# A decoder trunk on one Trainium2 core: Strassen products moved ahead of the memory's keys and values, memory outputs gated later on GpSimd, pooling issued in steps

## The chip, the core and the metric

The kernel runs on one core of a Trainium2 chip. The metric is the device time of one execution in microseconds (us), lower is better. A profile of one execution shows five engines: TensorE (PE, with its weight loads apart as PEld), VectorE (DVE), ScalarE (ACT), GpSimd (POOL) and SyncE (SP), which issues every transfer of this kernel. Each engine works through its own instructions in order.

## What is computed

Two layers over 1024 tokens of 1024 channels, all in float32. Layer 0 is the one that the change touches:

```python
h = x @ w_in                       # 1024 x 3072
u_main, q_mem = h[:, :1024], h[:, 1024:1536]
g_main, g_mem = h[:, 1536:2560], h[:, 2560:]
# pooling: 4 groups of 256 channels, trailing mean over w = 2, 4, 8, 16 tokens
pm     = trailing_mean(u_main, w) - u_main
y_main = (pm @ pool_w[group]) * pool_scale
# memory: 4 heads of 128, 256 memory tokens
y_mem  = softmax(q_mem @ mk.T / sqrt(128)) @ mv      # mk, mv = mem @ w_mem_kv
y      = concat(y_main * silu(g_main), y_mem * silu(g_mem)) @ w_out
x      = layer_norm(alpha * x + y)
```

Layer 1 has the same memory branch and projection, and forgetting attention of 16 heads instead of the pooling.

## The kernel before

Every float32 product is made of three matmuls on pairs of a rounded high half and a low remainder (`hi_lo`, L139 to L142: a cast on ScalarE, L141, and a subtraction on VectorE, L142). Activations lie with channels on the 128 partitions and tokens along the free axis.

Layer 0's projection is computed in **pairs** of 128-channel slabs by Strassen's scheme in Winograd's form (`winograd`, L194 to L246): seven products of 12 matmuls of 512 columns (L215) instead of eight. The right operands are x's four quarters and four sums of them, T1 to T4, made once by `sums_of_x` (L452 to L462: 16 subtractions on GpSimd, then 16 `hi_lo`). The left operands are a pair's weight quarters and four sums of these on GpSimd (L233 to L245), each split by `hi_lo` into two of the six `w` buffers. The first pair of slabs (`first_pair`, L464 to L486) has 96 plain matmuls (L478), because the sums of x are not there yet. There are eleven further pairs: one for the memory's queries (`mem_queries(2)`), six for gates (`gates_out` writes silu gates, doubled, to `gd` in DRAM; `pool_gates` either loads them or computes them in place), four for the pooled channels (`pool_in`).

`mem_kv` (L255 to L286) makes the memory's keys and values: 96 matmuls of 256 columns (L270) and 48 of 512 (L280), with weights cast and subtracted on the way (`split_w`, L151 and L152). `mem_attention` (L301 to L365) goes over eight blocks of 128 tokens: scores into the PSUM tile `L` (L171), exponentials and scalings on ScalarE (L321, L327), transposes (L294), and for each two blocks and each head a value product into `O`, which has one bank. `took` (L545) takes it out of `O`. Between these steps the `Fill` object issues matmuls of two gate pairs.

`pooled` (L554) makes a group's trailing mean on VectorE by log2(w) shifted additions of 1024 columns (L561) for each of two slabs, then subtracts, splits, and `pool_out` (L590) multiplies by the group's 256x256 weights (24 matmuls of 512 columns, L171 into `L`) and by the gate (L606) and stores to `y0d`. `out_proj` (L366) loads `y0d` by 512 KB tiles, chunk 2 (memory) first, then 0 (groups 0 and 1), then 1 (groups 2 and 3), and multiplies by w_out (L394).

What sets the order: TensorE's instructions of layer 0 stand in the order of the program text (`manual_schedule`); those of the other engines and the transfers are put in an order by a scheduler at build time, with the program text as priority, and buffers handed out in that order. The pools that matter have few buffers: `G` 4, `T` 6, `raw` 3, `raw2` 4, `P` 4, `Y` 2, `w` 6 and PSUM `pj` 3, `L` 2, `T` 2, `O` 1. A tile that finds no free buffer waits on its engine until one is released.

Of the kernel before, what the change touches and what calls it, by code (L numbers as in the profile page):

```python
# [16 lines left out]
P = 128  # L17
S = 1024
# [49 lines left out]
def trunk_kernel(ctx, tc, x, xT, memT, win, wk, wv0, wv, wmk, wmv, wout, poolw, pscale, lng, lnb, bforget, out):  # L68
# [25 lines left out]
    def sb(shape, tag, bufs, dt=F32, where=None):  # L94
        return (where or pool).tile(shape, dt, tag=tag, name=nm(tag), bufs=bufs)
# [7 lines left out]
    def T(shape=(P, S), dt=F32R):  # L103
        return sb(list(shape), "T", 6, dt)
# [4 lines left out]
    def raw(shape):  # L109
        return sb(list(shape), "raw", 3)  # L110
# [80 lines left out]

    SLAB = 48 * NH

    def winograd(w, X, banks, temps, out):  # L194

        f32, spare = temps

        def load(d, pc, t):
            nc.sync.dma_start(t, w[d][pc])
            return t

        def split(t):
            h, l = wt([P, 4, P]), wt([P, 4, P])
            hi_lo(h, l, t)
            return h, l

        def product(name, t, took):  # L210
            (h, l), (xh, xl) = split(t), X[name]
# [9 lines left out]
        def add(dst, a, b):  # L221
            nc.vector.tensor_tensor(dst, a, b, ALU.add)

        left, right = slice(0, NH), slice(NH, S)
        u = spare()
        u2, u3 = u[:, 0, :], u[:, 1, :]
        a11 = load(0, 0, f32())
        yield from product("B11", a11, lambda acc: nc.scalar.copy(u2, acc))
        a12 = load(0, 1, f32())
        yield from product("B21", a12, lambda acc: out(0, left, acc, u2))  # L230
        a21, a22 = load(1, 0, raw([P, 4, P])), load(1, 1, raw([P, 4, P]))
        s1, s2 = f32(), f32()
        nc.gpsimd.tensor_tensor(s1, a21, a22, ALU.add)  # L233
        nc.gpsimd.tensor_tensor(s2, s1, a11, ALU.subtract)
        yield from product("T2", s2, lambda acc: add(u2, acc, u2))
        nc.gpsimd.tensor_tensor(a21, a11, a21, ALU.subtract)
        yield from product("T3", a21, lambda acc: add(u3, acc, u2))
        yield from product("T4", a22, lambda acc: out(1, left, acc, u3))

        def fifth(acc):  # L240
            add(u2, acc, u2)
            out(1, right, acc, u3)

        yield from product("T1", s1, fifth)
        nc.gpsimd.tensor_tensor(s2, a12, s2, ALU.subtract)  # L245
        yield from product("B22", s2, lambda acc: out(0, right, acc, u2))  # L246

    PAIR = 84 * NH

# [182 lines left out]
    with tc.tile_pool(name="in0", bufs=1) as in0:  # L432
# [17 lines left out]
        place = (("B11", "T4"), ("B21", "B22"))  # L450

        def sums_of_x():  # L452
            for k in range(4):
                (b11, b12), (b21, b22) = ((t[:, 0, :], t[:, 1, :]) for t in (quarters[k], quarters[4 + k]))
                t12, t34 = (T((P, 2, NH), F32) for _ in range(2))
                t1, t2, t3, t4 = t12[:, 0, :], t12[:, 1, :], t34[:, 0, :], t34[:, 1, :]
                nc.gpsimd.tensor_tensor(t1, b12, b11, ALU.subtract)
                nc.gpsimd.tensor_tensor(t2, b22, t1, ALU.subtract)
                nc.gpsimd.tensor_tensor(t3, b22, b12, ALU.subtract)
                nc.gpsimd.tensor_tensor(t4, b21, t2, ALU.subtract)  # L460
                for n, t in (("T2", t2), ("T3", t3), ("T1", t1), ("T4", t4)):
                    hi_lo(X[n][0][:, k, :], X[n][1][:, k, :], t)  # L462

        def first_pair():  # L464

            accs = [[ps([P, NH], *b) for b in banks] for banks in ((("pj", 3), ("pj", 3)), (("pj", 3), ("L", 2)))]
            ws = {}
            for kt in range(KT):
                for d in range(2):
                    if kt % 4 == 0:  # L470
                        ws[d] = split_w(win[0, 8 + d, kt // 4], [P, 4, P])
                    if d == 0:
                        load_x(kt)
                    h, l = ws[d]
                    for n in range(2):
                        xh, xl = X[place[kt // 4][n]]
                        for i, (a, b) in enumerate(((h, xh), (h, xl), (l, xh))):
                            nc.tensor.matmul(  # L478
                                accs[d][n], a[:, kt % 4, :], b[:, kt % 4, :],
                                start=kt == 0 and i == 0, stop=kt == KT - 1 and i == 2,  # L480
                            )
            for d in range(2):
                for n in range(2):
                    t = T((P, 2, NH))
                    hi_lo(t[:, 0, :], t[:, 1, :], accs[d][n])
                    nc.sync.dma_start(qd[:, :, d, n * NH : (n + 1) * NH], t.bitcast(F32))  # L486

# [17 lines left out]

        qd = dram.tile([P, 2, MH, S], F32, name="qd")
        gd = dram.tile([P, 12, S], F32, name="gd")

        def mem_queries(h0):
            def out(d, cols, acc, add):  # L510
# [32 lines left out]
            return [(t[:, 0, h, :], t[:, 1, h, :]) for h in range(MH)]  # L543

        def took(c, h, acc):  # L545
            cols = slice(c * 2 * P, (c + 1) * 2 * P)
# [3 lines left out]
            nc.vector.tensor_tensor(chunk[0][:, h, :], acc, chunk[1][:, h, :], ALU.mult)  # L550
            if h == MH - 1:
                nc.sync.dma_start(y0d[2, :, :, cols], chunk[0])

        def pooled(g, us):  # L554

            w = WINDOWS[g]
            for u in us:
                cur, sh = u, 1
                while sh < w:
                    nxt = G()  # L560
                    nc.vector.tensor_tensor(nxt[:, sh:], cur[:, sh:], cur[:, : S - sh], ALU.add)  # L561
                    nc.vector.tensor_copy(nxt[:, :sh], cur[:, :sh])
                    cur, sh = nxt, 2 * sh
                pm = G()
                nc.vector.scalar_tensor_tensor(pm[:, w - 1 :], cur[:, w - 1 :], 1.0 / w, u[:, w - 1 :], ALU.mult, ALU.subtract)
                nc.vector.tensor_tensor(pm[:, : w - 1], cur[:, : w - 1], invc[:, : w - 1], ALU.mult)
                nc.vector.tensor_tensor(pm[:, : w - 1], pm[:, : w - 1], u[:, : w - 1], ALU.subtract)
                ph, pl = T(), T()
                hi_lo(ph, pl, pm)
                yield ph, pl  # L570

        def pool_in(g):
            us = [sb([P, S], "P", 4) for _ in range(2)]

            def out(d, cols, acc, add):
                nc.vector.tensor_tensor(us[d][:, cols], acc, add, ALU.add)

            run(pair(2 * g, out))
            return us

        def pool_gates(g):
            ys = [sb([P, S], "Y", 2, F32, in0) for _ in range(2)]
            if g < 2:
# [6 lines left out]
        def pool_out(g, pms, ys):  # L590
            r = raw([P, 2, 2 * P])
            nc.sync.dma_start(r, poolw[g])
            wh, wl = (MK([P, 2, 2 * P]) for _ in range(2))
            hi_lo(wh, wl, r)
            for d in range(2):
                f = 2 * g + d
# [382 lines left out]
```

## Time and profile before

| | before |
|---|---|
| runs, us | 1390.39, 1389.15, 1387.25; median 1389.15 |
| profiled execution, us | 1387.68, span 1386.0 |
| TensorE busy | 1317.9 us (95%) |
| VectorE, ScalarE, GpSimd busy | 834.2, 580.4, 366.6 us |
| mean granted TensorE clock | 0.983 |
| first pair | 5.65 to 28.1 us |
| memory's keys and values | 40.64 to 77.2 us |
| three pairs | 77.22 to 134.5 us |
| memory attention with two pairs | 139.38 to 230.9 us |
| pooling, six pairs | 230.90 to 371.15 us |

Times inside the profiled execution count from the start of its span. A group row gives line, engine, operation, tile written <- tiles read, then time; in square brackets stands the idle time of the engine ahead of the instruction and what ended it. The wait views count the same idle times by what was waited for. A granted clock of 1.00 is full speed.

### The profile page before, as it was taken

What the parts mean: (1) busy time and instruction counts of PE and PEld (TensorE: products, weight loads), DVE (VectorE), ACT (ScalarE), POOL (GpSimd) and SP (SyncE); (2) the same over time, 40 slices, a digit from 0 to 9 for tenths busy, and PEclk for the clock granted to TensorE, in tenths of its full rate; (3) what the DMA queues carried; (4) which work ended last, traced back from release to release, by engine and by line L of the source; (5) the groups of instructions that cost most, each with busy time, mean ns of one, the idle gap of its engine ahead of it and who ended that gap; (6) DMA issues with size and microseconds to landing.
All of it is one profiled execution on the core that took longest, in us unless ns stands there. A gap on an engine that the chain in (4) does not pass through costs nothing. (4 is left out here: it accounts for less than half of the span.)

```text
span 1386.0 us, 19391 instructions
## 1 busy us (share of the span) xinstructions
PE 1317.9 (95%) x6830; PEld 1108.0 (80%) x6830; DVE 834.2 (60%) x1675; ACT 580.4 (42%) x1239; POOL 366.6 (26%) x448
## 2 busy tenths in 40 slices
PE   7598889999999999999999999999999999999997
PEld 5477777787778888888988888888888888878886
DVE  5967645998856555255545555555555656675553
ACT  4543644223341124266325555555555555563110
POOL 0732111313000000000025455454545454622000
PEclk9799889999999999999999999999999999999999
DMA  7343444231473325111422132222222132365431
GB/s 250 107 160 114 129 139 143 71 120 54 152 251 119 106 98 171 47 31 30 149 63 70 54 92 75 78 83 64 90 57 90 54 92 70 114 199 191 136 121 46
DMA packets 82498, 148.29 MB, mean 107 GB/s; under 512 B 7904, under 2 KB 33760, under 8 KB 82400
## 3 DMA queue, kind: packets, MB, share of 16 engines
q1 hardware_dynamic: 82400, 147.04, 33.5%
q8 instruction: 54, 0.88, 0.3%
q14 instruction: 44, 0.36, 0.1%
HBM read 107.56 MB, written 31.06 MB: 100 GB/s over the span
## 5 line engine op out<-in xcount | busy, mean ns | idle before, releaser
L183 PE MATMUL pj<-A,w 128*128 128x512 f32 x1824 | 494.3, 402 | 0.8 <-DVE MK L142 0.8
L183 PEld LDWEIGHTS pj<-A,w 128*128 128x128 f32 x1824 | 320.6, 189 | 51.6 <-DVE MK L142 1.2
L142 DVE TENSOR_TENSOR T<-T,T 128x512 fp32r<-128x512 f32 (+2 forms) x248 | 151.9, 637 | 174.7 <-ACT T L141 117.6
L215 PE MATMUL pj<-A,w 128*128 128x512 f32 x924 | 219.8, 395 | 3.4 <-DVE w L142 3.4
L215 PEld LDWEIGHTS pj<-A,w 128*128 128x128 f32 x924 | 174.1, 191 | 39.5 <-DVE w L142 4.5
L141 ACT CAST T<-T 128x512 fp32r<-128x512 f32 (+2 forms) x252 | 131.2, 549 | 137.2 <-DMA T<-y1d 46.3
L807 ACT ACTIVATE P<-P,s 128x128 f32<-128x128 f32 (+7 forms) x128 | 99.6, 778 | 141.5 <-DVE s L805 140.6
L798 POOL TENSOR_SCALAR P<-R,cumn 128x128 f32<-128x128 f32 (+7 forms) x128 | 96.8, 756 | 210.8 <-PE T L294 153.1
L294 PE MATMUL T<-ident,P 128*128 128x128 f32 x704 | 101.5, 273 | 1.8 <-DVE V L142 1.1
L294 PEld LDWEIGHTS T<-ident,P 128*128 128x128 f32 x704 | 84.9, 140 | 20.8 <-DVE T L142 1.4
L141 ACT CAST w<-raw 128x512 fp32r<-128x512 f32 x81 | 50.3, 623 | 114.9 <-PE pj L215 103.1
L840 PEld LDWEIGHTS O<-T,V 128*128 128x128 f32 x640 | 85.0, 190 | 11.4 <-DVE T L142 5.2
L171 PE MATMUL L<-B,B 128*128 128x512 f32 (+3 forms) x384 | 89.0, 339 | 1.1 <-DVE s L805 1.1
L840 PE MATMUL O<-T,V 128*128 128x256 f32 (+1 forms) x640 | 85.3, 278 | 3.0 <-DVE T L142 2.7
L709 POOL MEMSET G<- 128x128 f32 x1 | 0.2, 206 | 322.2 <-DVE V L657 322.2
L171 PEld LDWEIGHTS L<-B,B 128*128 128x128 f32 x384 | 71.6, 188 | 17.1 <-DVE s L805 1.7
L805 DVE CUSTOM_DVE_ANT_0 P<-L,P 128x512 f32<-128x512 f32 (+3 forms) x128 | 72.7, 568 | 14.5 <-PE L L171 11.0
L152 DVE TENSOR_TENSOR w<-raw,w 128x512 fp32r<-128x512 f32 x58 | 45.5, 786 | 47.3 <-ACT w L151 47.1
L152 POOL TENSOR_TENSOR w<-raw,w 128x512 fp32r<-128x512 f32 x54 | 70.2, 1299 | 4.4 <-PE pj L183 0.9
L142 DVE TENSOR_TENSOR w<-raw,w 128x512 fp32r<-128x512 f32 x81 | 64.0, 792 | 11.2 <-ACT w L141 10.8
L846 DVE TENSOR_TENSOR G<-O,G 64x256 f32<-64x256 f32 x64 | 27.0, 422 | 71.6 <-ACT G L845 70.8
L151 ACT CAST w<-raw 128x512 fp32r<-128x512 f32 x58 | 36.0, 622 | 57.5 <-PE pj L183 26.9
(210 smaller groups left out, 1945.9 us busy)
## 6 DMA issues: line engine op xcount, KB each, us to landing
raw<-in_win_dram SPq DMA_DIRECT2D x96, 256.0 KB, 2.7
raw<-in_wout_dram SPq DMA_DIRECT2D x48, 256.0 KB, 3.1
B<-B SPq DMA_DIRECT2D x64, 128.0 KB, 2.5
R<-cumd SPq DMA_DIRECT2D x16, 512.0 KB, 3.7
y0d<-Y SPq DMA_DIRECT2D x12, 512.0 KB, 3.5
T<-y0d SPq DMA_DIRECT2D x12, 512.0 KB, 4.0
T<-y1d SPq DMA_DIRECT2D x12, 512.0 KB, 4.2
qd<-T SPq DMA_DIRECT2D x8, 512.0 KB, 3.8
```

Source lines behind the costliest of these rows:

```text
L141: nc.scalar.copy(hi, src)
L142: nc.vector.tensor_tensor(lo, src, hi.bitcast(F32), ALU.subtract)
L151: nc.scalar.copy(h, r)
L152: (nc.gpsimd if low[0] else nc.vector).tensor_tensor(l, r, h.bitcast(F32), ALU.subtract)
L171: nc.tensor.matmul(acc, a, b, start=i == 0, stop=i == len(terms) - 1)
L183: nc.tensor.matmul(accs[n], a[:, k, :], b[:, kt, n * NH : (n + 1) * NH], start=kt == 0 and i == 0, stop=kt == KT - 1 and i == 2,)
L215: nc.tensor.matmul(acc, a[:, k, :], b[:, k, :], start=k == 0 and i == 0, stop=k == 3 and i == 2)
L294: nc.tensor.transpose(t[:, j, :], src[:, (4 * g + j) * P : (4 * g + j + 1) * P], ident)
L798: nc.gpsimd.tensor_scalar(p[:, :L], R[:, :L], 1.0, cumn[:, i * HEADS + hd : i * HEADS + hd + 1], ALU.mult, ALU.add)
L805: nc.vector.tensor_tensor_reduce(p[:, lo:up], lg, p[:, lo:up], 1.0, top, ALU.add, ALU.min, m[:, n : n + 1])
L807: nc.scalar.activation(p[:, :L], p[:, :L], AF.Exp, bias=top, scale=-1.0, accum_out=sums[:, 8 * (hd % 2) + i : 8 * (hd % 2) + i + 1])
L840: nc.tensor.matmul(acc[:, w:], st, t[j // 4][:, j % 4, w:], start=j == 0 and e == 0, stop=j == last and e == 1,)
```

## The change

The order of layer 0 becomes: first pair, sums of x (T1 and T2 for all four k ahead of T3 and T4), memory queries, gates of group 3, pooled channels of group 3, gates 4 (memory), pooling of group 3 to its end, queries prefetched, keys and values, memory attention with gates 5 (memory) and gates of group 2 as filling, pooled channels of groups 2 and 1, group 2's output, memory outputs, gates of group 1, pooled channels of group 0, outputs of 1 and gates and output of 0. Before, it was first pair, keys and values, sums, queries, gates 4 and 5, memory attention with gates of groups 0 and 1 as filling, then groups 0 to 3.

- `winograd` issues all four weight loads at its start and splits each product's weights one product ahead; T1 comes ahead of T4.
- `took` only copies `O` to a `Y` tile on ScalarE and stores it to a new DRAM tensor `yraw`; `mem_out` later loads it and the gates in `G` tiles and multiplies them on GpSimd.
- `pooled` becomes a generator with a stop after each step; after each Strassen product two steps of it are issued (`chore(2)`), and `pool_out` finishes what is left.
- The first pair's query tiles go to the `Y` buffers instead of `T`, and the pooling weights to `w` instead of `MK`.

```diff
+    chores = []
+    def chore(n):
+        while n and chores:
+            if next(chores[0], chores) is chores:
+                chores.pop(0)
+            else:
+                n -= 1
...
+        a11, a12 = load(0, 0, f32()), load(0, 1, f32())
+        a21, a22 = load(1, 0, raw([P, 4, P])), load(1, 1, raw([P, 4, P]))
...
+        ahead = split(steps[0][1]())
+        for j, (name, _, took) in enumerate(steps):
+            (h, l), (xh, xl) = ahead, X[name]
+            if j < 6:
+                ahead = split(steps[j + 1][1]())
             acc = ps([P, NH], *banks)
...
                         took(acc)
+                        chore(2)
...
-                    t = T((P, 2, NH))
+                    t = sb([P, 2, NH], "Y", 2, F32R, in0)
...
-                chunk[0], chunk[1] = sb([P, MH, 2 * P], "Y", 2, F32, in0), G((P, MH, 2 * P))
-                nc.sync.dma_start(chunk[1], gd[:, 8:, cols])
-            nc.vector.tensor_tensor(chunk[0][:, h, :], acc, chunk[1][:, h, :], ALU.mult)
+                chunk[0] = sb([P, MH, 2 * P], "Y", 2, F32, in0)
+            nc.scalar.copy(chunk[0][:, h, :], acc)
             if h == MH - 1:
-                nc.sync.dma_start(y0d[2, :, :, cols], chunk[0])
+                nc.sync.dma_start(yraw[:, :, c * 2 * P : (c + 1) * 2 * P], chunk[0])
+        def mem_out():
+            for h in range(MH):
+                y, gt = G(), G()
+                nc.sync.dma_start(y, yraw[:, h, :])
+                nc.sync.dma_start(gt, gd[:, 8 + h, :])
+                for cols in (slice(0, NH), slice(NH, S)):
+                    nc.gpsimd.tensor_tensor(y[:, cols], y[:, cols], gt[:, cols], ALU.mult)
+                nc.sync.dma_start(y0d[2, :, h, :], y)
...
         first_pair()
-        kv = mem_kv(0)
         sums_of_x()
...
         run(mem_queries(2))
-        for f in (4, 5):
-            run(gates_out(f))
-        for f in (0, 1):
+        run(gates_out(3))
+        pms = pool_in(3)
+        run(gates_out(4))
+        pool_out(3, pms, pool_gates(3))
+        queries(0)
+        kv = mem_kv(0)
+        for f in (5, 2):
             fill.add(gates_out(f), PAIR)
         mem_attention(kv, queries, fill, took)
-        pms = list(pooled(0, pool_in(0)))
-        for g in range(4):
-            us = pool_in(g + 1) if g < 3 else None
-            pool_out(g, pms, pool_gates(g))
-            if g < 3:
-                pms = list(pooled(g + 1, us))
+        pms2 = pool_in(2)
+        pms1 = pool_in(1)
+        pool_out(2, pms2, pool_gates(2))
+        mem_out()
+        ys = pool_gates(1)
+        pms0 = pool_in(0)
+        pool_out(1, pms1, ys)
+        pool_out(0, pms0, pool_gates(0))
```

More of the change, by code (lines that the diff above doesn't have):

```diff
@@ L208, in split, with add, less, sums @@
             return h, l
-        def product(name, t, took):
-            (h, l), (xh, xl) = split(t), X[name]
+        def add(dst, a, b):
+            nc.vector.tensor_tensor(dst, a, b, ALU.add)
+        def less(dst, a, b):
+            nc.gpsimd.tensor_tensor(dst, a, b, ALU.subtract)
+            return dst
+        left, right = slice(0, NH), slice(NH, S)
+        u = spare()
+        u2, u3 = u[:, 0, :], u[:, 1, :]
+        a11, a12 = load(0, 0, f32()), load(0, 1, f32())
+        a21, a22 = load(1, 0, raw([P, 4, P])), load(1, 1, raw([P, 4, P]))
+        s1, s2 = f32(), f32()
+        def sums():
+            nc.gpsimd.tensor_tensor(s1, a21, a22, ALU.add)
+            return less(s2, s1, a11)
+        def fifth(acc):
+            add(u2, acc, u2)
+            out(1, right, acc, u3)
+        steps = (
+            ("B11", lambda: a11, lambda acc: nc.scalar.copy(u2, acc)),
+            ("B21", lambda: a12, lambda acc: out(0, left, acc, u2)),
+            ("T2", sums, lambda acc: add(u2, acc, u2)),
+            ("T3", lambda: less(a21, a11, a21), lambda acc: add(u3, acc, u2)),
+            ("T1", lambda: s1, fifth),
+            ("T4", lambda: a22, lambda acc: out(1, left, acc, u3)),
+            ("B22", lambda: less(s2, a12, s2), lambda acc: out(0, right, acc, u2)),
+        )
+        ahead = split(steps[0][1]())
[3 more added lines that the diff above has]
+                ahead = split(steps[j + 1][1]())
             acc = ps([P, NH], *banks)
@@ L218, in product @@
                         took(acc)
+                        chore(2)
                     yield NH
[L221 to L246, printed above, removed]
     PAIR = 84 * NH
@@ L452, in sums_of_x @@
         def sums_of_x():
+            t12s = []
             for k in range(4):
                 (b11, b12), (b21, b22) = ((t[:, 0, :], t[:, 1, :]) for t in (quarters[k], quarters[4 + k]))
[L455 to L456 removed]
+                t12s.append(T((P, 2, NH), F32))
+                t1, t2 = (t12s[k][:, j, :] for j in range(2))
                 nc.gpsimd.tensor_tensor(t1, b12, b11, ALU.subtract)
                 nc.gpsimd.tensor_tensor(t2, b22, t1, ALU.subtract)
+                for n, t in (("T2", t2), ("T1", t1)):
+                    hi_lo(X[n][0][:, k, :], X[n][1][:, k, :], t)
+            for k in range(4):
+                (b11, b12), (b21, b22) = ((t[:, 0, :], t[:, 1, :]) for t in (quarters[k], quarters[4 + k]))
+                t34 = T((P, 2, NH), F32)
+                t3, t4 = t34[:, 0, :], t34[:, 1, :]
                 nc.gpsimd.tensor_tensor(t3, b22, b12, ALU.subtract)
[L460 to L461 removed]
+                nc.gpsimd.tensor_tensor(t4, b21, t12s[k][:, 1, :], ALU.subtract)
+                for n, t in (("T3", t3), ("T4", t4)):
                     hi_lo(X[n][0][:, k, :], X[n][1][:, k, :], t)
@@ L507, in trunk_kernel @@
         gd = dram.tile([P, 12, S], F32, name="gd")
+        yraw = dram.tile([P, MH, S], F32, name="yraw")
         def mem_queries(h0):
@@ L563, in pooled @@
                     cur, sh = nxt, 2 * sh
+                    yield
                 pm = G()
@@ L578, in pool_in @@
             run(pair(2 * g, out))
-            return us
+            pms = []
+            chores.append(pooled(g, us, pms))
+            return pms
         def pool_gates(g):
             ys = [sb([P, S], "Y", 2, F32, in0) for _ in range(2)]
-            if g < 2:
+            if g > 1:
                 for d in range(2):
@@ L590, in pool_out @@
         def pool_out(g, pms, ys):
+            while len(pms) < 2:
+                chore(1)
             r = raw([P, 2, 2 * P])
             nc.sync.dma_start(r, poolw[g])
-            wh, wl = (MK([P, 2, 2 * P]) for _ in range(2))
+            wh, wl = (wt([P, 2, 2 * P]) for _ in range(2))
             hi_lo(wh, wl, r)
```

7 lines of the change are left out of this document (4 added, 3 removed).

## Prediction

> **What bounds the kernel now.** I read the page's sections 1 and 2 first, then TensorE's waits over the whole span, then stages, then timelines. Section 1's engines and section 2's rows of TensorE and its clock:
>
> ```profile
> PE 1317.9 (95%) x6830; PEld 1108.0 (80%) x6830; DVE 834.2 (60%) x1675; ACT 580.4 (42%) x1239; POOL 366.6 (26%) x448
> PE   7598889999999999999999999999999999999997
> ...
> PEclk9799889999999999999999999999999999999999
> ```
>
> The longest of TensorE's waits (total, times, longest):
>
> ```profile
> PE O L171 <- DVE Y L550: 13.0, 6, 6.5
> PE pj L270 <- ACT w L151: 12.3, 1, 12.3
> PE pj L270 <- DVE w L152: 9.3, 7, 2.5
> PE L L171 <- DMA G<-qd: 4.9, 1, 4.9
> ```
>
> TensorE sets the end, and its waits of any size lie in slices 1 to 10, layer 0, which is all that the change touches. The stages of that layer:
>
> ```profile
> 28.00:77.00 49.00, 27.27 (x146) 22.43 (x145) 40.25 (x45) 23.80 (x44) 25.46 (x16) 0.83 0.46 145
> 77.00:134.00 57.00, 57.00 (x253) 47.22 (x252) 40.87 (x55) 22.55 (x37) 19.56 (x15) 1.00 0.40 130
> 139.00:231.00 92.00, 78.00 (x425) 66.85 (x426) 54.41 (x115) 50.40 (x136) 10.30 (x8) 0.90 0.43 134
> 231.00:371.00 140.00, 133.57 (x577) 108.60 (x576) 120.76 (x178) 43.03 (x67) 32.60 (x20) 0.99 0.30 97
> ```
>
> After the window come length, busy time of PE, PEld, DVE, ACT, POOL, granted clock, DMA share and GB/s. Both programs have 6822 matmuls, so I count each stage's **excess**, its time less its matmuls at full clock: 0.227 us for 512 columns (252 in 57.28 us), 0.141 for 256 (24 in 3.39). Memory keys and values: 28.1 to 77.2 is 49.1, work 96x0.141 + 48x0.227 = 24.4, excess 24.7. The wait for queries: 4.9. Memory attention: 139.4 to 230.9 is 91.5; work 168x0.227 + 8x1.43 for scores + 16x0.72 for values + 8x0.79 for transposes = 67.3; excess 24.2, of which 13.5 are waits and the rest mostly the clock after them. Pooling: 230.9 to 371.15 is 140.3, work 576x0.227 = 130.8, excess 9.5. Together 63.3 us to win from.
>
> **The start.** The memory's keys and values leave the place after the first pair, and with them the waits of 12.3 and 8.4 us on L270. The next pair's products stand there instead. What is late next is VectorE: in the built order the low half of that pair's first weights stands behind all 16 sums of x and their splits, two evacuations too. The fifth x tile, with which the second-quarter sums can begin, lands at 12.2 (ACT's cast of G). From there VectorE has 33 operations of 512 columns up to that split, GpSimd 15 subtractions or additions that it waits for or competes with. What they cost each other is in these rows, VectorE's three and then GpSimd's two:
>
> ```profile
> 41.56 1.75 DVE L142 TENSOR_TENSOR A<-T,A 128x512 fp32r<-128x512 f32 x1
> 43.23 0.68 DVE L152 TENSOR_TENSOR w<-raw,w 128x512 fp32r<-128x512 f32 x1
> 43.83 1.75 DVE L142 TENSOR_TENSOR A<-T,A 128x512 fp32r<-128x512 f32 x1
> ...
> 41.16 1.59 POOL L458 TENSOR_TENSOR T<-G,T 128x512 f32<-128x512 f32 x1
> 43.38 1.66 POOL L459 TENSOR_TENSOR T<-G,P 128x512 f32<-128x512 f32 x1 [0.63 <-DVE A L142]
> ```
>
> Beside a GpSimd operation VectorE steps 1.68 us, in GpSimd's gap 0.62: they take turns, and one GpSimd operation costs VectorE 1.06. So the split ends at 12.2 + 33x0.62 + 15x1.06 = 48.6. Bounds: 12.2 + 33x0.62 + 2 + 15x0.15 = 37 if GpSimd costs almost nothing (its own 15 operations at 1.29 end at 31.6), 52 if it costs a whole 1.29. I take 48.6, since both queues are full there as in the rows. The Trainium skill, SBUF — State Buffer, section Who interferes with whom, has the loser blocked until the whole other instruction ends. By that the price is 1.29 and the split ends at 52.0, not 48.6; the rows show 1.06, and I keep them. The first pair itself, without waits now after 6.4, will stutter behind the same queue (its last x split is VectorE's 27th operation, near 35) and end near 41; that is inside the 48.6. After a TensorE gap of that length the clock is half:
>
> ```profile
> 193.00:196.00 3.00, 0.00 (x0) 0.00 (x0) 0.95 (x2) 0.46 (x1) 0.00 (x0) 0.50 0.93 296
> 196.00:199.00 3.00, 2.78 (x10) 2.49 (x11) 0.59 (x2) 0.00 (x0) 0.00 (x0) 0.50 0.35 122
> 199.00:202.00 3.00, 3.00 (x12) 2.61 (x11) 0.68 (x2) 0.62 (x1) 0.00 (x0) 0.50 0.00 0
> ```
>
> Work of 3.3 took 6.1 us after the 6.5 us wait, and 4.6 for 2.9 after one of 2.1. I add 2.5. Excess 48.6 - 28.1 + 2.5 = 23.0.
>
> **Keys and values in their new place.** They stand after pool_out(3). Their second weight load waits on the sync queue behind the store of pool_out(3)'s last output, then takes 2.5 us to land, 0.6 + 0.7 to split; 12 matmuls of the first weight cover 1.7. That leaves 3.6, with clock and the eight value slabs (0.8 and 0.3 waited in layer 1) 6.0; bounds 1 and 9.
>
> **Memory attention.** Queries are prefetched ahead of the keys: the 4.9 goes, with 2.6 of slow clock after it. The product of gates goes from VectorE (L550, 0.42) and its gate load with it; a copy on ScalarE takes its place (L845 shows such a copy from O). The one-bank tile O is still freed before the next head. In the built order ScalarE copies head 0, then four exponentials, a tanh and four scalings, then head 1. After head 0's matmuls end at 188.7 that queue ran:
>
> ```profile
> 188.80 0.47 ACT L321 ACTIVATE P<-L,s 128x256 f32<-128x256 f32 x1 [1.69 <-PE O L171]
> 190.61 0.64 ACT L501 ACTIVATE G<-G 128x512 f32<-128x512 f32 x1
> 191.24 1.71 ACT L327 ACTIVATE P<-P,s 128x256 f32<-128x256 f32 x4
> ```
>
> So with head 0's copy (0.45) ahead, head 1's ends at 194.0, while TensorE is ready for head 2 at 191.5: 2.6 us, in three of four chunks, each with 1.5 of slow clock; bounds 0 and 4.3. The Trainium skill, TensorE: Matmul & The Clock Gate, Part 1, lets the clock fall only after an idle window of about 3.4 us. By it the 1.5 would be nothing here and the sum 4.5 lower; the trace has 0.50 at 346 to 348 after a wait of 2.13, though not after one of 2.28 at 363. The last chunk keeps its 2.9, and I let 2.5 of today's unexplained rest stay: 3x4.1 + 2.9 + 2.5 = 17.7.
>
> **Pooling.** VectorE's pooling of group 3 is 12 operations of 1.14 (1024 columns), small ones 1.5; gates pair 4, beside it, brings 18 of 0.64. Before, two pairs were there to hide it. Now pool_out(3) follows one pair (19.1): VectorE needs 13.7 + 1.5 + 11.5 + 4 GpSimd operations at 0.75 = 30, and stays busy until then, so TensorE waits first for the last weights, then for the pooled tile: 11.7 with clock, bounds 8 and 14. Group 2 beside pair 1 the same way: 20.2 + 3 against 19.1, 4.0. Between the gates of group 1 and pair 0, the first weight split of pair 0 stands behind group 1's pooling and the last gate's tanh: at least 0.7 + 1.1 + 3x0.62 = 3.7 after the last product. But mem_out comes in: its eight 512 KB loads and four stores hold all four G buffers, each of which pooling and tanh need next, and the loads of pair 0's weights stand behind its first store on the sync queue. A load lands in about 4, two GpSimd products take 2.6 to 3.3, a store 3.7: followed load by load, these put the split 8 us after the last product instead of 3.7; with 1.5 of clock 9.5, bounds 4 and 14. Group 0 beside the last gates fits (21.5 against 24.8). With 2.0 for evacuations before the L bank: 27.2.
>
> **Into the projection.** The last outputs are now groups 0 and 1, which the projection reads second, not last: store 3.5, load 4 to 5, cast and split 2.3 make 11 to 12 after the last product, against 44 matmuls (10.0). 2.0, bounds 0 and 4. The products of memory and gate on GpSimd are else hidden by pair 0.
>
> Sum after: 23.0 + 6.0 + 17.7 + 27.2 + 2.0 = 75.9, before 63.3: **12.6 slower**, 1387.68 + 12.6 = 1400.3 beside the profiled execution. The runs' median, 1389.15, is 1.5 above it, so 1401.8.
>
> **Rivals.** (1) *GpSimd's price is low.* In the pooling stage the weight splits average 823 ns against 685 alone, all such rows some 11 us for 20 GpSimd operations: 0.55 each. At 0.55 the start is 7.6 shorter, group 3, pair 1 and mem_out about 1, 2 and 2: no change. That is where it decides; at 0.3 it is 11.4 + 2 + 3 + 5 = 21 less, 1381, faster. Against it: VectorE was not always full there, but will be at the start. 0.22. (2) *Copies on ScalarE come in time*, because exponentials run before head 0 ends: 12.3 less, 1389.5. Against it is the order shown. 0.10. (3) *The sync queue in order costs more*: mem_out's loads and stores delay the weights of two pairs, not one; 10 more, 1412. 0.12. That the change does not do what it says is excluded by the built order. My forecast: 0.56.
>
> **Chances.** Faster than before by over 0.2% (2.8 us, about what a measurement of this kernel tells from no change): 0.22; within: 0.07, most of rival 2; slower 0.71. The range reaches to 1381 and, with the upper bounds, 1418.
>
> **What would show it.** Right: TensorE's first product of the second pair near 48, waiting for a VectorE weight split; a wait of 4 to 6 us ahead of pool_out(3); O waits now on ScalarE, three of 2 to 3 us; pair 0's first product waiting 4 us or more; no wait of over 6 us in keys and values. Wrong: that product before 40, or pooling stages without waits of over 3 us.

## The result and the profile after

The changed kernel takes 1406.19 us, median of 4 runs (1404.56 to 1408.48); the kernel before, beside it, 1389.29 (4 runs, 1387.25 to 1390.39). The ratio is 1.0125, 95% interval [1.0106, 1.0143]: slower by 17 us, where 12.6 were predicted (1401.8). The profiled execution's span is 1404.3 us, 18.3 longer than before, with the granted clock at 0.979.

Sections 1 and 2 of its page, the same rows as before:

```profile
PE 1329.2 (95%) x6830; PEld 1114.8 (79%) x6830; DVE 831.3 (59%) x1659; ACT 583.4 (42%) x1255; POOL 383.2 (27%) x456
...
PE   7897888986999999999999999999999999999997
...
PEclk9999999998999999999999999999999999999999
```

The number of matmuls is unchanged and their time longer by 11.3 us: part of the loss is slow clock. The dips of TensorE still lie in slices 1 to 10, but slices 9 and 10 (281 to 351 us, pooling), full before, now hold 8 and 6, and the tenth a clock of 8. TensorE's longest waits, total, times, longest (line numbers are each kernel's own: L259 here is L215 of the kernel before, L503 is L478, L288 is L270; L574 is the copy out of `O`, L601 the last step of pooling, L646 the gate on an output):

```profile
PE O L171 <- ACT Y L574: 10.2, 6, 3.5
PE pj L259 <- DVE w L142: 9.0, 5, 3.7
PE pj L259 <- DVE G L601: 8.8, 1, 8.8
PE L L171 <- ACT T L141: 5.1, 1, 5.1
PE pj L503 <- DVE A L142: 4.3, 5, 1.7
PE pj L259 <- DVE Y L142: 3.9, 1, 3.9
```

The waits of 12.3 and 8.4 us of layer 0's keys and values and the queries' 4.9 are gone; in their new place keys and values wait 3.1 and 1.0. New are waits of the pairs for VectorE (weight splits, pooling on L601, first pair's halves on Y), and pool_out(3)'s wait for the cast of its pooled tile. The O waits (TensorE ahead of a value product, until the one bank of `O` has been taken out) are now for ScalarE's copy, and 10.2 instead of 13.0. By stages, in the prediction's unit (time less matmuls at full clock), the two traces give:

| stage | before | predicted after | measured after |
|---|---|---|---|
| keys and values, queries; in after the start: 28.1 to 123.3, 326 matmuls | 24.7 + 4.9 | 23.0 | 21.2 |
| keys and values, new place: 141.85 to 171.65 | | 6.0 | 5.4 |
| memory attention: 171.65 to 260.62 | 24.2 | 17.7 | 21.7 |
| pooling, group 3: 123.3 to 141.85 | | 11.7 | 10.8 |
| pooling, the rest: 260.62 to 396.54 | 9.5 | 15.5 | 23.3 |
| into the projection | | 2.0 | 0 |
| sum | 63.3 | 75.9 | 82.4 |

To the end of the last pool_out that is 19.1 more, of which 0.4 is before's own last pool_out; at layer 1's keys (L288 against L270) 18.7 are left, at the end 18.3. So the loss is one of pooling, 34.1 against 9.5; what the start, the keys and the attention win back is 5.5. The start on TensorE:

```profile
41.01 0.84 PE L503 MATMUL L<-A,w 128*128 128x512 f32 x3
45.80 1.22 PE L259 MATMUL pj<-A,w 128*128 128x512 f32 x2 [3.95 <-DVE Y L142]
48.19 2.08 PE L259 MATMUL pj<-A,w 128*128 128x512 f32 x4 [1.17 <-DVE w L142]
```

The first pair ends at 41.85, the second starts in earnest at 48.19, behind the weight split: predicted 41 and 48.6. The pooling stages on TensorE:

```profile
133.22 0.80 PE L171 MATMUL L<-T,w 128*128 128x512 f32 x1 [5.14 <-ACT T L141]
...
299.56 3.97 PE L259 MATMUL pj<-A,w 128*128 128x512 f32 x10 [2.25 <-DVE w L142]
...
339.17 1.19 PE L259 MATMUL pj<-A,w 128*128 128x512 f32 x2 [8.83 <-DVE G L601]
344.05 20.78 PE L259 MATMUL pj<-A,w 128*128 128x512 f32 x82 [3.69 <-DVE w L142]
```

The first row is pool_out(3), the second pair 1 beside group 2, the last two are pair 0, behind mem_out. After the wait of 8.83 the granted clock is 0.50; in the windows of 339 to 348 (window, length, busy PE, PEld, DVE, ACT, POOL, clock, DMA, GB/s) TensorE holds 12 matmuls, 2.7 us of work:

```profile
339.00:342.00 3.00, 1.19 (x2) 0.50 (x2) 2.93 (x6) 2.90 (x5) 0.00 (x0) 0.50 0.00 0
342.00:345.00 3.00, 0.95 (x2) 0.83 (x3) 3.00 (x6) 0.80 (x2) 0.00 (x0) 0.50 0.00 0
345.00:348.00 3.00, 3.00 (x8) 2.31 (x7) 0.20 (x1) 0.00 (x0) 1.27 (x1) 0.50 0.41 103
```

Over 339 to 365, 86 matmuls (19.5 us of work) kept TensorE busy for 22.1: 2.6 us of slow clock on top of 12.5 of waits, where the prediction had 9.5 in all.

### The profile page after: what moved, and what is told of

Read it like the earlier page. It is cut to its first block, busy times and chain, and to the rows that moved or that the text cites. A ratio compares the mean times of both kernels' runs of the same rounds, so it can differ in the third digit from the quotient of the medians.

```text
span 1404.3 us, 19418 instructions
## 1 busy us (share of the span) xinstructions
PE 1329.2 (95%) x6830; PEld 1114.8 (79%) x6830; DVE 831.3 (59%) x1659; ACT 583.4 (42%) x1255; POOL 383.2 (27%) x456
## 4 chain that ended last, share of the span: by engine, by line
PE 60%; DVE 7%; DMA 4%; ACT 3%; issue 2%; POOL 1%; DVEq 0%; SPq 0%; ACTq 0%; POOLq 0%
PE pj L183 25%; PE pj L412 8%; PE L L412 7%; PE T L312 5%; PE L L171 4%; PE O L885 4%; PE pj L259 2%; DMA raw<-in_wout_dram 2%; PE pj L725 2%; DVE P L850 1%; ACT P L852 1%; DVE T L142 1%; PE O L171 1%; DMA raw<-in_wmv_dram 1%; POOL P L843 1%
## 5 line engine op out<-in xcount | busy, mean ns | idle before, releaser
L259 PE MATMUL pj<-A,w 128*128 128x512 f32 x924 | 224.6, 400 | 22.2 <-DVE w L142 9.0
L259 PEld LDWEIGHTS pj<-A,w 128*128 128x128 f32 x924 | 175.9, 193 | 61.4 <-DVE w L142 11.7
L141 ACT CAST w<-raw 128x512 fp32r<-128x512 f32 x85 | 52.6, 621 | 111.5 <-PE pj L259 87.9
L142 DVE TENSOR_TENSOR w<-raw,w 128x512 fp32r<-128x512 f32 x85 | 64.1, 759 | 24.8 <-ACT w L141 24.6
L224 POOL TENSOR_TENSOR raw<-raw,raw 128x512 f32<-128x512 f32 x33 | 47.9, 1458 | 105.5 <-DVE w L142 64.5
L152 DVE TENSOR_TENSOR w<-raw,w 128x512 fp32r<-128x512 f32 x58 | 41.8, 725 | 51.7 <-ACT w L151 51.4
```

Source lines behind the costliest of these rows:

```text
L141: nc.scalar.copy(hi, src)
L142: nc.vector.tensor_tensor(lo, src, hi.bitcast(F32), ALU.subtract)
L152: (nc.gpsimd if low[0] else nc.vector).tensor_tensor(l, r, h.bitcast(F32), ALU.subtract)
```

## The experiments

Theory: the loss comes from VectorE being full where the new order puts pooling beside too few pairs, and from mem_out standing ahead of pair 0; the start costs what VectorE's queue and its turns with GpSimd make it. Rivals: GpSimd's part is cheap, the sync queue is the cause, or the keys' new place is itself a loss. The kernel before took 1387.7 to 1388.5 us (medians) beside these runs.

**1. Sums of x on VectorE.** The changed kernel with

```diff
-                nc.gpsimd.tensor_tensor(t1, b12, b11, ALU.subtract)
+                nc.vector.tensor_tensor(t1, b12, b11, ALU.subtract)
```

and the same for t2, t3 and t4.

> The changed kernel with the 16 sums of x on VectorE instead of GpSimd. Theory (the start is bound by VectorE's queue, in which a GpSimd operation costs 1.06 us and one of its own 0.62): the first weight split of the second pair ends 4 to 5 us earlier than the 48.1 of the changed kernel, and the whole is about 1401. Rival (the start is bound by the loads of x or by ScalarE's casts): the split ends within 1 us of 48 and the time stays at 1406. A second rival (GpSimd's share is nearly free): the split ends later, at 50 or more, and the time is about 1409.

Measured: 1402.04 us, ratio 1.0094 [1.0070, 1.0118]. Its start on TensorE:

```profile
32.57 0.73 PE L259 MATMUL pj<-A,w 128*128 128x512 f32 x2 [2.15 <-DVE Y L142]
43.46 6.74 PE L259 MATMUL pj<-A,w 128*128 128x512 f32 x19 [10.16 <-DVE w L142]
```

As the theory had it: the split is 4.7 us earlier although VectorE has 16 operations of 0.60 to 0.62 more. Taking these 9.8 off, it would stand near 33.6 with the sums free, so GpSimd's 15 or 16 operations cost VectorE 14.5 us, 0.9 to 1.0 each. Predicted was 1.06; rival 1's 0.55 is out. The split shows this better than the times do, whose ratios' intervals, this one and the changed kernel's, touch.

**2. Memory outputs later.** The changed kernel with mem_out behind pair 0:

```diff
-            mem_out()
             ys = pool_gates(1)
             pms0 = pool_in(0)
+            mem_out()
```

> The changed kernel with mem_out placed after pool_in(0) instead of before the gates of group 1. Theory (the waits of 8.8 and 3.7 us at the start of pair 0 come from mem_out's tiles holding the four G buffers that pooling and tanh of group 1 need): the two together fall to 3 to 5 us, no new wait as long elsewhere, and the whole is 1396 to 1400. Rival (VectorE has too much pooling there by itself): the two stay above 9 us and the time stays within 3 of 1406. Second rival (the buffers are only missed later): the waits go from pair 0 but 5 us or more come back at the last outputs or at the projection.

Measured: 1399.67 us, 1.0082 [1.0066, 1.0098]. Pair 0's 8.83 and 3.69 are gone; one wait of 3.45 for a weight split is left, in the gates of group 1 ahead of it. But mem_out now holds its buffers beside group 0's pooling, and pool_out(1) waits 4.24 for an output product (L646), with slow clock: 5.44 for 12 matmuls, 2.7 of work.

```profile
360.40 5.44 PE L171 MATMUL L<-T,w 128*128 128x512 f32 x12 [4.24 <-DVE Y L646]
```

Net 6.5 us less. The time and pair 0 are as the theory said; that some 7 us came back at a later output is the second rival's.

**3. Two pairs beside group 3.** The changed kernel with

```diff
             run(gates_out(4))
+            run(gates_out(5))
             pool_out(3, pms, pool_gates(3))
...
-            for f in (5, 2):
+            for f in (1, 2):
```

and `pool_gates` loading the gates for g above 0.

> The changed kernel with one more pair (gates 5) between the pooled channels of group 3 and its output, and the gates of group 1 as filling in memory attention in its place; gates of group 1 are then loaded. Theory (the waits of 1.5 and 5.6 us and the slow clock at pool_out(3), 10.9 in all, are pooling that one pair cannot cover; the gates of group 1 no longer stand behind mem_out): the wait ahead of pool_out(3) falls under 1 us, that at pair 0 under 5, and the whole is 1388 to 1394. Rival (the work on VectorE only moves its stall to the next place): the sum of TensorE's waits in layer 0 falls by less than 5 us and the time is over 1400.

Measured: 1395.72 us, 1.0057 [1.0038, 1.0076]. pool_out(3)'s 5.14 is gone (0.49 is left), though gates 4 now wait 3.35 for a weight split, 1.53 in the changed kernel. Gone are pair 0's two waits too, though mem_out is where it was: the gates of group 1 are now filling, and pair 0 follows pool_out(2) directly. What mem_out delays is now pool_out(1), the next thing on VectorE:

```profile
345.29 0.49 PE L171 MATMUL L<-T,w 128*128 128x512 f32 x1 [2.16 <-ACT w L141]
...
352.12 5.78 PE L171 MATMUL L<-T,w 128*128 128x512 f32 x16 [5.38 <-DVE w L142]
```

10.5 us less, between the theory and its rival. By stages, group 3's excess falls from 10.8 to 5.8 and that of the rest of pooling from 23.3 to 18.3: some 5 us each. The edit moves two things, gates 5 beside group 3 and the gates of group 1 away from mem_out, and the time does not part them.

**4. Keys and values moved, nothing else.** The kernel before with

```diff
-            kv = mem_kv(0)
             sums_of_x()
...
             for f in (4, 5):
                 run(gates_out(f))
+            kv = mem_kv(0)
```

> The kernel before with one edit: the memory's keys and values after the gates 4 and 5 instead of ahead of the sums of x. Theory (the waits of keys and values are only exchanged for a wait for the sums and splits on VectorE and GpSimd): the first product of the second pair starts at 44 to 52, keys and values take about 26 to 30 us in their new place, and the whole is 1384 to 1394. Rival (the place was the loss): second pair before 40, and the time 1370 to 1380.

Measured: 1378.04 us, 0.9926 [0.9906, 0.9945]: faster by 9.7, as the rival had it. The second pair on TensorE, and the keys in their new place:

```profile
28.34 6.28 PE L215 MATMUL pj<-A,w 128*128 128x512 f32 x27
...
55.94 6.35 PE L215 MATMUL pj<-A,w 128*128 128x512 f32 x16 [0.93 <-DVE w L142]
```

```profile
107.73 7.35 PE L270 MATMUL pj<-T,w 128*128 128x256 f32 x60
...
133.59 1.60 PE L171 MATMUL L<-MK,G 128*128 128x256 f32 x12
```

Here two products of the second pair run at once, then TensorE waits for sums until 55.9. Keys and values take 25.9 us, an excess of 1.5 against 24.7 in their old place, the start 22.2 (28.3 to 107.7, 252 matmuls), and the queries' wait is gone: 23.7 for 29.6. The memory attention, with less slow clock at its start, has 21.0 for 24.2. The profiled spans differ by 7.5, the medians by 9.7. The move is a gain; the loss is in the rest of the change.

**5. Where the sums stand.** In the trace of run 4 the weight splits stand ahead of the sums, in the changed kernel behind them. The reason is a buffer: `first_pair` writes its query halves to Y instead of T, T is free at once, and the sums start during the first pair. The changed kernel with that undone:

```diff
-                    t = sb([P, 2, NH], "Y", 2, F32R, in0)
+                    t = T((P, 2, NH))
```

> The changed kernel with one line undone: first_pair's query halves are split into two tiles of T again instead of Y. In the changed kernel the sums of x start at 8.2 us, because T is free, and their VectorE splits stand among and ahead of the first pair's own. In the order built here the four tiles of the first pair hold T until its evacuations, so the sums and their 16 splits stand behind the first weight splits of the second pair. Theory (it is this buffer, not the order of the sums in the text, that puts the second pair's weight split behind the sums): first pair ends near 28 to 29, second pair's first product at 28 to 30 without a wait for a weight split; sums of T1 and T2 done near 43, all near 55, so that some 48 matmuls lie in the gap and TensorE is continuous from about 55; the start then ends some 3 us earlier: 1400 to 1405 us. Rival (where the sums stand does not matter, GpSimd's 16 operations are the bound either way): the end of the three pairs stays within 1 us of 123.3, time 1405 to 1408.

Measured: 1406.97 us, 1.0133 [1.0114, 1.0151]: the rival. TensorE, then VectorE's splits of the sums:

```profile
29.75 5.83 PE L259 MATMUL pj<-A,w 128*128 128x512 f32 x25
...
46.52 4.62 PE L259 MATMUL pj<-A,w 128*128 128x512 f32 x10 [9.52 <-DVE w L142]
54.35 1.21 PE L259 MATMUL pj<-A,w 128*128 128x512 f32 x2 [3.22 <-ACT w L141]
57.93 4.32 PE L259 MATMUL pj<-A,w 128*128 128x512 f32 x11 [2.37 <-DVE w L142]
```

```profile
32.38 12.41 DVE L142 TENSOR_TENSOR A<-T,A 128x512 fp32r<-128x512 f32 x8
44.72 1.75 DVE L142 TENSOR_TENSOR w<-raw,w 128x512 fp32r<-128x512 f32 x1
46.39 10.29 DVE L142 TENSOR_TENSOR A<-T,A 128x512 fp32r<-128x512 f32 x8
```

Two products earlier, but all sums 10 us later: 38 matmuls are done by 57.9, and the changed kernel has done 39 by then. My theory had forgotten that T2's weight split stands behind all eight splits of T1 and T2, and T3's product behind the rest. Either order pays the turns of 16 sums, most of which take GpSimd 1.6 to 1.7 us instead of 1.3: one in the first pair and ahead of the second pair's weights, the other inside the second pair.

**6. Run 4 with the new order of the sums** (T1 and T2 of all four k first, the hunk of `sums_of_x` in the change).

> The kernel before with two parts of the change alone: keys and values moved behind the gates of 4 and 5, and sums of x with T1 and T2 of all four k ahead of T3 and T4. Moved alone it was 1378.0, with 24 matmuls of the second pair done at 28 to 36 us and TensorE continuous from 55.9. Theory (the sums' end on GpSimd bounds the start, and what matters is how many matmuls are done before it): T2's product can run from about 43 and T3's between 45 and 55, some 24 matmuls more in the gap, 5 us less: 1371 to 1375 us. Rival (T3 and T4 end as late as before and VectorE's splits are what the products wait for, so the order of the sums gives nothing): 1377 to 1381 us.

Measured: 1380.06 us, 0.9940 [0.9918, 0.9962]. No gain over run 4's 0.9926: the rival, with the same wait as in run 5, 9.51 us for T2's weight split at 46.85.

**7. Gating later, nothing else.** The kernel before with the change's `took`, and mem_out behind `mem_attention`.

> The kernel before with one part of the change alone: memory outputs copied out of O on ScalarE, stored, and multiplied by the gate on GpSimd by mem_out right behind the memory attention; nothing else is changed. Theory from my prediction: memory attention wins 2 to 3 us (O waits 10 instead of 13), but mem_out's twelve transfers and the G buffers stand in the way of the next pooling pair and its weights, 4 to 9 us: 1390 to 1396 us, slower by 2 to 7. Rival (the cost of mem_out came from its place between two short covers in the changed kernel; behind the attention it is hidden): 1384 to 1388 us.

Measured: 1390.41 us (10 runs), 1.0013 [1.0002, 1.0024]: some 2 us slower, at the lower edge of the theory. Both terms of its sum are there, and both are larger than it had them: the O waits fall from 13.0 to 4.5 us, where 10 was expected, and the pair behind mem_out waits 8.89 and 2.91 for weights. That their difference fits is luck in part.

```profile
PE O L171 <- ACT Y L549: 4.5, 6, 2.2
```

```profile
253.43 1.22 PE L215 MATMUL pj<-A,w 128*128 128x512 f32 x2 [8.89 <-ACT w L141]
257.57 16.31 PE L215 MATMUL pj<-A,w 128*128 128x512 f32 x58 [2.91 <-DVE w L142]
```

**8. Run 3 with the gate applied at once** (the old `took`, no mem_out).

> The run e4_cover_group3 (1395.7 us) with one part of the change undone: memory outputs are multiplied by the gate on VectorE as they leave O, as in the kernel before, and mem_out is gone. Gates 4 and 5 both lie ahead of the memory attention in that order, so the gates are there. Theory: O waits go back from 10 to 13 us (3 more), the waits of pool_out(1) and of pair 1 behind mem_out (2.2 and 5.4 with slow clock) go: 1388 to 1393 us. Rival (gating later is a net gain, and the pooling waits stay, coming from the pairs' order): 1396 to 1402 us.

Measured: 1387.13 us (10 runs), 0.9990 [0.9974, 1.0006], 8.6 less than run 3, just below the theory's range and far from the rival's. pool_out(1) and the gates of group 0 behind it, here without the waits shown in run 3:

```profile
347.20 2.88 PE L171 MATMUL L<-T,w 128*128 128x512 f32 x12
350.55 3.01 PE L171 MATMUL L<-T,w 128*128 128x512 f32 x12 [0.46 <-DVE Y L648]
353.40 19.20 PE L259 MATMUL pj<-A,w 128*128 128x512 f32 x84
```

The O waits are 12.1. By stages, gating at once costs 4.2 us in the memory attention (25.4 for run 3's 21.2) and saves 11 in the pooling behind it (7.1 for 18.3). So with run 3's order and the gating as before, the change's loss of 17 us is gone.

**9. Pooling in one go.** The changed kernel with

```diff
-            chores.append(pooled(g, us, pms))
+            for _ in pooled(g, us, pms):
+                pass
```

> The changed kernel with one part undone: the pooling of a group is issued in one go behind its pair, not in steps after each later product. The widest group still comes first. Theory (the built order of VectorE mixes pooling and weight splits in either case, since splits wait for their buffers; what costs time is that 12 operations of 1.14 us and 18 of 0.64 do not fit beside one pair, and that is unchanged): 1403 to 1409 us, the waits ahead of pool_out(3) and pair 0 as in the changed kernel. Rival (the steps keep weight splits from standing behind pooling, and without them the pair after each pool_in waits for weights, up to 4 us for each of four groups): 1410 to 1420 us.

Measured: 1411.51 us, 1.0157 [1.0131, 1.0182], 5.3 more than the changed kernel by the medians: the rival, though the two ratios' intervals overlap a little. Gates 4 now wait 8.19 in their fifth product behind group 3's pooling (L601), and pool_out(3) no longer waits; later pair 0 waits 8.91 in its second product and pool_out(1) 3.74. The steps are worth some 5 us in this order.

**10. Sync queue or G buffers.** The changed kernel with

```diff
-                nc.sync.dma_start(y0d[2, :, h, :], y)
+                nc.gpsimd.dma_start(y0d[2, :, h, :], y)
```

> The changed kernel, with mem_out's four stores issued from GpSimd's queue, right behind the multiplications that they wait for, instead of from SyncE. The loads of pair 0's weights no longer stand behind those stores; the four G buffers are still held by mem_out. Before pair 0 the changed kernel waits 8.8 and 3.7 us. Theory (mine, the sync queue: the loads of pair 0's weights wait in order behind the stores of mem_out and of the gates): one or both of these waits fall to 4 us together at most, 1398 to 1402 us. Rival (the G buffers: tanh and pooling of VectorE, which stand ahead of the weight split, wait for a G buffer until mem_out has stored it): the waits stay within 2 us of 12.5, 1404 to 1408 us, or a little more for the issue on GpSimd.

Measured: 1404.26 us, 1.0107 [1.0088, 1.0126], not told apart from the changed kernel. The 168 matmuls of group 1's gates and pair 0 on TensorE, of which 60 are done ahead of the first row; then one instruction each of VectorE, ScalarE and SyncE from the time of the waits:

```profile
332.48 1.20 PE L259 MATMUL pj<-A,w 128*128 128x512 f32 x2 [5.52 <-DVE P L221]
339.68 25.98 PE L259 MATMUL pj<-A,w 128*128 128x512 f32 x106 [6.01 <-DVE w L142]
```

```profile
321.75 1.23 DVE L594 TENSOR_TENSOR G<-P 128x1023 f32<-128x1023 f32 x1 [4.54 <-POOL G L584]
```

```profile
327.53 0.63 ACT L526 ACTIVATE G<-Y 128x512 f32<-128x512 f32 x1 [5.61 <-POOL G L584]
```

```profile
321.15 1.85 SPq L212 DMA_DIRECT2D raw<-in_win_dram  x4
```

The four weight loads are issued together at 321.15, instead of two at 323.62 and two at 327.07. The two waits have moved from pair 0 into the gates ahead of it and still sum to 11.5 us, against 12.5. Pooling (L594) and tanh (L526) each wait for a G buffer that mem_out's product (L584) holds, and VectorE's weight splits stand behind them. The buffers decide, not the place of the stores in the queue (mem_out's loads stay on SyncE).

**11. A version from what was learned.** Run 4 with the sums of x on VectorE, the halves in Y, the first two weight splits of the second pair ahead of the sums in the text, the change's look-ahead, and one adder tile in T (`next` issues the loads and splits of B11 and B21):

```diff
-            sums_of_x()
...
+            second = mem_queries(2)
+            next(second)
+            sums_of_x()
...
-            run(mem_queries(2))
+            run(second)
```

> A version built from what the runs showed, on the kernel before with keys and values moved (1378.0 us): sums of x on VectorE (no turns with GpSimd), first pair's halves in Y as in the changed kernel, so that sums start during the first pair, and the first two weight splits of the second pair ahead of the sums in the text, with the look-ahead of the changed kernel and the adder tile of that one pair in T. Theory: VectorE has about 51 operations of 0.62 us from 12.2 to the last sum's split, near 44; 24 matmuls of the second pair are done by then; TensorE continuous from about 45.5 instead of 55.9 with as many done, 10 us less: 1366 to 1371 us. Rival (look-ahead and Y give part of it back in the later pairs or the first pair stutters by more than 2 us): 1372 to 1379 us.

Measured: 1374.55 us, 0.9894 [0.9870, 0.9918]; 1366 to 1371 were expected, and this is the rival's range. The start itself came as worked out:

```profile
33.03 7.83 PE L251 MATMUL pj<-A,w 128*128 128x512 f32 x26 [2.55 <-DVE Y L142]
45.73 16.62 PE L251 MATMUL pj<-A,w 128*128 128x512 f32 x60 [4.88 <-DVE w L142]
```

TensorE is continuous from 45.7, and memory attention starts at 125.2 instead of 133.6 in run 4, 8.4 us earlier. Of that the medians keep 3.5, the profiled spans 7.1; the O waits rose from 11.9 to 13.3. What takes the rest in the median is open.

**12. Run 11 with the gate loads of `took` on GpSimd's queue.**

```diff
-                nc.sync.dma_start(chunk[1], gd[:, 8:, cols])
+                nc.gpsimd.dma_start(chunk[1], gd[:, 8:, cols])
```

> The version f6_sums_early_on_vector (1374.55 us) with the four gate loads of the memory outputs issued from GpSimd's queue instead of SyncE's. In f6 two of the O waits (3.2 and 5.4 us) end with VectorE's product of the first head, whose gate load is issued late: the second stands behind weight loads that SyncE waits 6.8 us for. Theory (the sync queue's order makes these loads late): both fall under 1.5 us, with the slow clock after them 6 to 9 us less: 1365 to 1369 us, so that the cheap cure for the O waits was a queue and not a copy on ScalarE with the gating later. Rival (the G buffer, or GpSimd's own waits ahead of the load, make them late): O waits stay at 11 to 14 us, 1372 to 1377 us.

Measured: 1372.13 us, 0.9897 [0.9863, 0.9931]. The rival: O waits 12.0. The loads come earlier (the second is issued at 167.7, where SyncE issued it at 173.9), but the longest wait only fell from 5.44 to 4.87, since the product stands on VectorE behind the next weight split:

```profile
173.85 0.69 DVE L142 TENSOR_TENSOR w<-raw,w 128x512 fp32r<-128x512 f32 x1 [1.51 <-ACT w L141]
174.46 0.41 DVE L561 TENSOR_TENSOR Y<-O,G 128x256 f32<-128x256 f32 x1
```

Runs 11 and 12 both beat both kernels, by some 1% of the kernel before; between the two the measurement does not decide.

## Why the prediction was right, and where it was not

**The start: right.** 48.6 was predicted and 48.19 measured, through the queue named and near the price named (run 1: 0.9 to 1.0 per GpSimd operation, 1.06 assumed). That it came so near is luck in part: one price stands for turns that cost between nothing and 1.1 us, and VectorE was not full to the end, but stood idle for 1.83 us ahead of the last two splits of sums, waiting for ScalarE's cast of a late sum. Rival 1, the only faster one, fell with it. The Trainium skill, SBUF — State Buffer, section Who interferes with whom, has whoever loses the shared port blocked for the whole of the other's instruction. By that the price was 1.29 and the split at 52.0; run 1's 0.9 to 1.0 and the 48.19 do not agree.

**Keys and values: right in size, 5.4 for 6.0.** The second weight's load stands behind pool_out(3)'s last store, as said (issued at 143.43, the store at 143.01), and costs 2.24; 1.87 more were waited for the first weight, which the sum had not. But I set the old place's 29.6 against 29.0 for start and new place together, as if the move were worth nothing. Alone, it is worth 9.7 us (run 4). The sum missed little by that, because the change's own start gives a part back (21.2 + 5.4 = 26.6 against 23.7 in run 4).

**Memory attention: the waits right, the rest mis-sized.** Three O waits of 3.49, 2.21 and 3.15 on ScalarE were measured (predicted three of 2.6), the last chunk 1.4 (2.9). The slow clock came to some 4.5, as predicted, though not evenly: the windows after the first, second and third long wait are

```profile
205.00:208.00 3.00, 2.98 (x10) 2.69 (x11) 0.00 (x0) 0.37 (x1) 0.00 (x0) 0.50 0.09 33
...
227.00:230.00 3.00, 3.00 (x22) 2.74 (x21) 2.14 (x4) 2.14 (x5) 2.60 (x2) 1.00 0.01 3
...
246.00:249.00 3.00, 2.41 (x9) 2.21 (x10) 0.00 (x0) 0.92 (x3) 0.00 (x0) 0.50 0.23 87
249.00:252.00 3.00, 3.00 (x14) 2.81 (x13) 0.00 (x0) 0.37 (x1) 0.00 (x0) 0.50 0.00 0
```

that is 1.5, 0 and, to 252.6, 2.9. The step that failed is "I let 2.5 of today's unexplained rest stay": 21.7 less 10.2 of O waits and 4.5 of clock leaves 7.0. I had put before's rest down to the clock; here 2.5 of it are five small waits of 0.3 to 1.0. The other 4.5 is spread over the timeline in steps of at most 0.5 us, most of them in the rows next to a wait; what makes them stays open. Rival 2, copies that come in time, is out in the changed order; in the old one (run 7) the O waits did fall to 4.5.

**Pooling: the mechanism right, its largest term too small.** Group 3 took 10.8 (11.7), with the chain named: weights, then the pooled tile; run 3 halved it by a second pair. Pair 1 took 2.6 of waits and 2.1 of slow clock (4.0 predicted). The mis-sized term is mem_out ahead of pair 0: 9.5 predicted, 12.5 of waits and 2.6 of clock measured. Of its two causes, G buffers and sync queue, run 10 leaves the buffers: GpSimd's four pairs of products wait for loads, and each keeps a G tile that tanh and pooling need in turn. Rival 3, the sync queue, would have been hardly further off in the total (1412) by the wrong cause.

**Into the projection: wrong, 0 instead of 2.0.** The two kernels are as far apart ahead of the projection (19.1 less before's 0.4) as at layer 1's keys behind it, 18.7 us; its waits of 0.4 to 0.5 are as small as before's.

Together: start and keys 2.4 too high, attention 4.0 and pooling 6.9 too low, projection 2.0 too high, which turns 12.6 into 19.1; less 0.4 of before's last pool_out and 0.4 in layer 1, this is the span's 18.3. So the total is nearer than its terms: 4.4 too much cancels against 10.9 too little.

The change as a whole is then one good part (keys moved, 9.7 us), one that costs some 2 in the old order and 8.6 in that of run 3 (gating later), and an order that puts the widest pooling beside one pair and the gates of group 1 behind mem_out (10.5 for both together); the steps are worth some 5. These do not add up to 17, since the parts act on each other. Run 8, with the loss gone, is still 9 us behind run 4: by stages 5.9 for group 3, 4.4 in the memory attention and 3.4 in the keys and values, of which the start and the rest of pooling give some 5 back. No run took that apart.

## What to carry to other kernels

A stage that hides another engine's work hides just as much as its own time: before moving pooling, splits or gates, add up that engine's instructions per stage and set them against the stage's matmuls. Work that is moved off the busy engine still holds buffers; if these belong to the pool from which the busy engine takes its next tile, its queue stops at the first request. Try the parts of a change alone: here one was worth 9.7 us and the whole cost 17.

## What was not expected of the hardware

VectorE and GpSimd do not always take turns. In the changed kernel, VectorE's splits and GpSimd's sums from 30 to 43 us:

```profile
30.97 4.17 DVE L142 TENSOR_TENSOR A<-G,A 128x512 fp32r<-128x512 f32 x5
35.06 5.50 DVE L142 TENSOR_TENSOR A<-T,A 128x512 fp32r<-128x512 f32 x9
```

```profile
35.88 5.82 POOL L484 TENSOR_TENSOR T<-G,P 128x512 f32<-128x512 f32 x1 [3.70 <-DVE A L142]
41.66 1.26 POOL L485 TENSOR_TENSOR T<-G,T 128x512 f32<-128x512 f32 x1
```

Nine VectorE operations ran one behind the other at 0.61 each, while one GpSimd operation that takes 1.26 alone needed 5.82. In run 5 eight of the same VectorE operations, with GpSimd running one operation after another beside them, took 1.55 each. Which side pays seems to hang on whose next instruction is ready, and no run was made for that alone.

The clock fell to 0.50 after waits of 3.49 and 3.15 us and stayed at 1.00 after one of 2.21 in the same stage; it had fallen after one of 2.13 in the kernel before. In run 3, with the same three waits (3.48, 2.21 and 3.14), it was the other way about: 0.50 after the wait of 2.21, 1.00 after that of 3.14. The Trainium skill, TensorE: Matmul & The Clock Gate, Part 1, has the window of 3.4 us run freely, not from the start of the wait. The trace agrees that the wait's length alone does not settle it, and does not agree that it takes a whole window: in both kernels it fell after less.
